# A transformer block and a two-layer mixer on one core: two-operand work moved from Pool to VectorE, and the feed-forward norm's root applied behind the up-products

## The chip, the core and the metric

One core of a Trainium2 chip runs the whole program. Its engines are TensorE (PE in the profile; its weight loads are PEld), VectorE (DVE), ScalarE (ACT), GpSimd (POOL, called Pool here) and SyncE (SP), which issues most DMAs. The metric is the device time of one execution in microseconds, as the median of several runs. Beside it there is one profiled execution, with every instruction's start and duration.

## What is computed

512 tokens of 1024 features go through a first block (mixer and feed-forward) and then through two layers of a second block. All is float32. Cut to what the change touches:

```python
def rms_norm(x, g):
    return x * lax.rsqrt(jnp.mean(x * x, axis=-1, keepdims=True) + 1e-6) * g

# first block
h = rms_norm(x, norm_mix_pre); proj = h @ w_in        # queries, keys, values, pool, memory queries, gates
mix = gate0 * y_attn + gate1 * y_pool + gate2 * y_mem
x = x + rms_norm(mix @ w_out, norm_mix_post)
h2 = rms_norm(x, norm_ffn_pre)
up = causal_depthwise_conv(h2 @ w_up, conv_w, conv_b)  # 3 taps along the tokens, 2 x 2816 features
g, v = split(up); ff = (gelu(g) * v) @ w_down
x = x + rms_norm(ff, norm_ffn_post)
# second block, layer 0: attention of 16 heads over the tokens and 256 context tokens, rotary positions, silu gates
# second block, layer 1: neighbourhood attention of 8 heads beside a depthwise convolution of 31 taps, a layer norm
#   and silu; then the last norm
```

The root of `h2`'s norm is one number for each token. A product over the features commutes with it: (x g r) @ W = r ((x g) @ W).

## The kernel before, in words

Features lie on the 128 partitions, tokens along the free dimension: x is 8 tiles of 128 x 512. Every weight product (`Product`, line 438) makes one 128 x 512 tile of results. It loads 128 x 1024 weights (`raw`), splits them into a high part on ACT (`whi`, line 458) and a low part, `raw - whi` (`wlo`, line 460), and makes 8 x 3 matmuls: high by high, high by low, low by high. Moving operands are split in the same way (`split`, line 488, `split_scaled`, line 492). Two buffers each hold the weights' parts, so the split of one product lies beside the matmuls of the product before it.

PE works in program order, and the program is written out by a planner in Python that counts microseconds of matmuls (`clock`). `advance`, `steps` and `run` issue matmuls of a batch; `defer(us, f)` calls f after so many microseconds of them; `background` holds work of other engines, given out at `rate` items per microsecond; `weave` puts products between the steps of attention; `drain` gives out the rest. The other engines take their instructions in their own order, DVE and Pool among them, and DMAs are issued by SP in order (a few by ACT).

Pool has these two-operand operations before the change: weights' low parts wherever `low_parts_on(G)` holds (lines 693 to 701 and 1541 to 1545: the start, and the latents' attention of layer 0); every third block's square sum with `SumSq(T, True)` (line 552); low parts of every third block in `norm_to` (line 582); the sums of the multiscale pool (line 717); the mix's additions (line 851); six of eight additions to x in `post_norm` (line 1418); two of four rotary products (lines 1068, 1070); gating and low parts in `lat_apply` (lines 1517, 1518); the last 13 of 31 taps of the depthwise convolution (`NTAP`, lines 1711 to 1717), each an ACT copy with a scale and a Pool addition to `ub`, which line 1723 merges; two sums of the layer norm (line 1731); every third product of the last norm (line 1787). Pool also has operations with one tensor operand, which stay: the scaling of scores by their sums (lines 775, 921, 1131) and of the bias (line 1648).

At the end of the first block's mixer the output products run (`outs`), then `post_norm` adds their normed result to x block by block, then the second root is made (`rms_now`, line 571: sums over the features on PE, nine small DVE steps in `rsqrt`, a spread by PE) and `norm_to` makes `h2` from x, gain and root. Meanwhile PE does the context's products (`filler`). Then x is stored to DRAM (`spill_x`), and the 44 up-products, 24 down-products and the context's attention follow, woven. An up-product's result is taken up by `conv3`: ACT scales it and adds the bias, and two DVE operations add the earlier tokens' taps, all three from PSUM:

```python
            S.activation(out=o, in_=ps, func=AF.Identity, scale=vc("conv_w", 88 + ct), bias=vc("conv_b", ct))
            V.scalar_tensor_tensor(out=o[:, 1:], in0=ps[:, :T - 1], scalar=vc("conv_w", 44 + ct), in1=o[:, 1:],
                                   op0=ALU.mult, op1=ALU.add)
```

Two PSUM banks take products' results at that time (`set_banks(2, 2)`).

Of the kernel before, what the change touches and what calls it, by code (L numbers as in the profile page):

```python
# [14 lines left out]
ALU = mybir.AluOpType  # L15
# [16 lines left out]
NTAP = 13   # convolution taps on the Pool engine  # L32
# [160 lines left out]
class Blocks:  # L193
    """[128, kt, n] as a tile for each of the kt blocks"""
# [8 lines left out]
def body(nc, tc, A, out, dbg=None):  # L203
# [75 lines left out]
    lo_engines = deque()  # L279

    def low_parts_on(*engines):
        lo_engines.clear()
        lo_engines.extend(engines)

    low_parts_on(V)
# [31 lines left out]
    # Products come in batches, which run in the order in which they were added. The weights of the next two are under way  # L317
    # while one runs.
# [69 lines left out]
    def lazy(weights, n, products):  # L388
        """the products of these weights, which products() gives when the first one starts"""
# [12 lines left out]
    def when(ready, products):  # L402
        """the products, not before ready()"""
# [21 lines left out]
    def need(ready):  # L425
        """more of the woven batch until ready()"""
# [4 lines left out]
    # ------------------------------------------------ products in three passes of float32r parts  # L431
# [6 lines left out]
    class Product:  # L438
        """one tile of a product, then evac(psum). cols: columns of the operand; keep: (pool, buffers) for the weights'
        parts; same: an earlier product with the same weights"""  # L440
# [11 lines left out]
        def parts(self):  # L452
            if self.same:
                self.hi, self.lo = self.same.hi, self.same.lo
            elif self.hi is None:
# [3 lines left out]
                lo_engines.rotate(-1)  # L459
                lo_engines[-1].tensor_tensor(out=self.lo[:, :n], in0=self.raw[:, :n], in1=f32(self.hi[:, :n]), op=ALU.subtract)  # L460
# [27 lines left out]
    def split(src, hi, lo, eng=None):  # L488
        S.copy(out=hi, in_=src)  # L489
        (eng or V).tensor_tensor(out=lo, in0=src, in1=f32(hi), op=ALU.subtract)  # L490
# [8 lines left out]
    def token_sums(accs, n, sel=None):  # L499
        """accs, each [128 features, n tokens] -> sums over the features (by the columns of sel), tokens on partitions"""  # L500
# [1314 lines left out]
```

## Time and profile before

| | us |
|---|---|
| three runs | 1807.56, 1810.9, 1818.63 |
| median | 1810.9 |
| profiled execution, first to last instruction | 1808.9 |
| PE busy / DVE busy / ACT busy / POOL busy in it | 1684.3 / 1278.4 / 902.7 / 390.0 |

Of the profiled execution's own time the profile gives the span alone. Busy time of an engine is the time in which at least one of its instructions ran; successive instructions of one engine overlap a little in the record, and matmuls are pipelined, so PE's busy time is not PE at its peak. PEclk is the share of the full TensorE clock that was granted.

### The profile page before, as it was taken

Reading aid. Unit: us, or ns where it says so; the run is one execution under the profiler, and the core shown is the slowest. Engines: PE = TensorE matmul, PEld = TensorE weight load, DVE = VectorE, ACT = ScalarE, POOL = GpSimd, SP = SyncE. Lnnn points to the kernel's source line nnn. Section 1 sums busy time; section 2 is a strip of 40 time slices with the busy share of each in tenths; the row PEclk is TensorE's granted clock in tenths of the full one; section 3 lists DMA queues with packets and bytes.
Section 4 is the critical chain, followed back from the end, with each engine's and each line's share of the span. In section 5 each row is a group of like instructions: output and inputs, shape, how many; then the busy total and the mean of one; then the engine's idle time right before and its main releaser. Section 6 shows DMA issues by size and latency. Waiting matters only on the chain. (4 is left out here: it accounts for less than half of the span.)

```text
span 1808.9 us, 25065 instructions
## 1 busy us (share of the span) xinstructions
PE 1684.3 (93%) x8756; PEld 1407.0 (78%) x8756; DVE 1278.4 (71%) x2474; ACT 902.7 (50%) x1700; POOL 390.0 (22%) x364
## 2 busy tenths in 40 slices
PE   7899999999998889999999998999988989888797
PEld 7788888888776768888778777778877787777677
DVE  6678766777597676644664767677778667888774
ACT  5443225555423456654763433366767445565452
POOL 3320111010021210000000002145544004656400
PEclk8999999999999999999999999999999999999898
DMA  5435555544364432333333556232321554243141
GB/s 197 136 121 176 162 164 151 135 122 117 126 202 161 148 103 94 123 118 105 111 100 110 193 163 211 84 103 70 78 64 47 186 172 137 82 120 97 35 140 59
DMA packets 84878, 227.10 MB, mean 126 GB/s; under 512 B 12048, under 2 KB 24720, under 8 KB 84752
## 3 DMA queue, kind: packets, MB, share of 16 engines
q1 hardware_dynamic: 82880, 220.51, 39.3%
q10 hardware_dynamic: 1872, 4.98, 0.9%
q8 instruction: 70, 1.15, 0.3%
q14 instruction: 56, 0.46, 0.1%
HBM read 181.93 MB, written 9.44 MB: 106 GB/s over the span
## 5 line engine op out<-in xcount | busy, mean ns | idle before, releaser
L294 PE MATMUL mm<-hh,whi 128*128 128x512 f32 (+1 forms) x1120 | 442.2, 395 | 16.6 <-DVE tg L593 4.6
L458 ACT CAST whi<-raw 128x1024 fp32r<-128x1024 f32 (+2 forms) x264 | 268.4, 1017 | 378.7 <-PE mm L294 326.8
L294 PE MATMUL mm<-hh,wlo 128*128 128x512 f32 (+1 forms) x1120 | 424.1, 379 | 6.4 <-DVE wlo L460 6.4
L294 PE MATMUL mm<-hl,whi 128*128 128x512 f32 (+1 forms) x1120 | 424.5, 379 | 3.4 <-DVE hl L490 1.7
L460 DVE TENSOR_TENSOR wlo<-raw,whi 128x1024 fp32r<-128x1024 f32 (+2 forms) x245 | 309.9, 1265 | 151.1 <-ACT whi L458 147.2
L294 PEld LDWEIGHTS mm<-hh,whi 128*128 128x128 f32 x1120 | 216.6, 193 | 51.4 <-DVE tg L593 6.1
L294 PEld LDWEIGHTS mm<-hh,wlo 128*128 128x128 f32 x1120 | 215.2, 192 | 48.8 <-DVE wlo L460 7.8
L294 PEld LDWEIGHTS mm<-hl,whi 128*128 128x128 f32 x1120 | 216.3, 193 | 34.2 <-DVE hl L997 2.7
L1131 POOL TENSOR_SCALAR sb<-sb,l 128x256 f32<-128x256 f32 (+3 forms) x128 | 106.3, 832 | 453.8 <-DVE l L1130 377.6
L294 PE MATMUL mm<-h2h,whi 128*128 128x512 f32 x352 | 141.8, 403 | 4.0 <-DVE cv L1342 3.0
L490 DVE TENSOR_TENSOR ptl<-tr,pth 128x512 fp32r<-128x512 f32 (+2 forms) x240 | 115.6, 497 | 41.8 <-ACT pth L489 40.0
L489 ACT CAST pth<-tr 128x512 fp32r<-128x512 f32 (+2 forms) x240 | 100.3, 436 | 89.8 <-PE tr L586 88.3
L294 PE MATMUL mm<-h2l,whi 128*128 128x512 f32 x352 | 140.1, 398 | 3.5 <-POOL h2l L490 2.1
L294 PE MATMUL mm<-h2h,wlo 128*128 128x512 f32 x352 | 139.7, 397 | 0.8 <-DVE wlo L460 0.8
L586 PE MATMUL tr<-c,sb 128*128 128x128 f32 x624 | 107.5, 282 | 25.1 <-DVE ptl L490 12.8
L586 PEld LDWEIGHTS tr<-c,sb 128*128 128x128 f32 x624 | 78.9, 145 | 52.0 <-issue 10.3
L810 DVE CUSTOM_DVE_ANT_0 mj<-mraw,cb 128x1024 f32<-128x1024 f32 x88 | 111.1, 1263 | 1.2 <-DMA mraw<-in_mod_w 0.5
L1126 ACT ACTIVATE sb<-sb,mn 128x512 f32<-128x512 f32 (+1 forms) x64 | 49.7, 776 | 70.7 <-DVE mn L1122 51.6
L1710 DVE SCALAR_TENSOR_TENSOR mixf<-up,vec,mixf 128x512 f32<-128x512 f32 x68 | 80.9, 1189 | 1.0 <-ACT mixf L1708 0.2
L294 PEld LDWEIGHTS mm<-h2l,whi 128*128 128x128 f32 x352 | 66.4, 189 | 19.2 <-POOL h2l L490 3.2
L294 PEld LDWEIGHTS mm<-h2h,whi 128*128 128x128 f32 x352 | 66.3, 188 | 19.2 <-issue 4.0
L1717 POOL TENSOR_TENSOR ub<-ub,ta 128x512 f32<-128x512 f32 x48 | 78.9, 1644 | 7.8 <-ACT ta L1716 5.1
(374 smaller groups left out, 3303.6 us busy)
## 6 DMA issues: line engine op xcount, KB each, us to landing
raw<-in_w_in SPq DMA_DIRECT2D x56, 512.0 KB, 3.4
mraw<-in_mod_w SPq DMA_DIRECT2D x48, 512.0 KB, 3.4
raw<-in_w_up SPq DMA_DIRECT2D x44, 512.0 KB, 3.4
raw<-in_ev_w SPq DMA_DIRECT2D x40, 512.0 KB, 3.4
raw<-in_od_w SPq DMA_DIRECT2D x36, 512.0 KB, 3.5
qd<-hl SPq DMA_DIRECT2D x48, 256.0 KB, 5.1
raw<-in_w_d SPq DMA_DIRECT2D x16, 512.0 KB, 3.3
raw<-in_ev_o SPq DMA_DIRECT2D x16, 512.0 KB, 3.4
```

The source lines that it names most:

```text
L294: on_pe(nc.tensor.matmul(ps, l, r, start=start, stop=stop), max(n * 0.00042, 0.107) * (2 if l.dtype == F32 else 1))
L458: S.copy(out=self.hi[:, :n], in_=self.raw[:, :n])
L460: lo_engines[-1].tensor_tensor(out=self.lo[:, :n], in0=self.raw[:, :n], in1=f32(self.hi[:, :n]), op=ALU.subtract)
L489: S.copy(out=hi, in_=src)
L490: (eng or V).tensor_tensor(out=lo, in0=src, in1=f32(hi), op=ALU.subtract)
L586: on_pe(nc.tensor.transpose(out=ps[:, k * P:(k + 1) * P], in_=src(b), identity=ident), 0.107)
L810: tc.keep_in_program_order(V.tensor_tensor_reduce(out=jk, in0=raw, in1=cb[:, n, :], scale=0.5, scalar=0.0, op0=ALU.mult, op1=ALU.add, accu ...
L1126: S.activation(out=sb, in_=src, func=AF.Exp, scale=-1.0, bias=mn, accum_out=l[:, 0:1])
L1131: G.tensor_scalar(out=sb, in0=sb, scalar1=l[:, 0:1], scalar2=0.0, op0=ALU.mult, op1=ALU.add)
L1710: V.scalar_tensor_tensor(out=u[m], in0=up[:, j:j + T], scalar=wc(j), in1=u[m], op0=ALU.mult, op1=ALU.add)
L1717: G.tensor_tensor(out=st["ub"], in0=st["ub"], in1=pj, op=ALU.add)
```

## The change

It does two things. First, all two-operand work of Pool named above is VectorE's; `low_parts_on`, `NTAP`, the second accumulator of `SumSq` and the `eng` argument of `split` are gone, and all 30 taps of the depthwise convolution after the first are one DVE chain. A very small copy in the multiscale pool goes the other way, from VectorE to Pool. Second, `post_norm` makes `h2`'s parts from x and the gain alone, in the same loop, and the root multiplies each up-product's result in `conv3`; results that come before the root wait in `unrooted`. With it, the filler runs to its end before x is stored, `h2` and the feed-forward's accumulator take the first block's buffers (`hp`), and the table `base` is loaded before the differential attention rather than at the start. (Comments are gone too.)

```diff
 Product.parts
-                lo_engines.rotate(-1)
-                lo_engines[-1].tensor_tensor(out=self.lo[:, :n], in0=self.raw[:, :n], in1=f32(self.hi[:, :n]), op=ALU.subtract)
+                V.tensor_tensor(out=self.lo[:, :n], in0=self.raw[:, :n], in1=f32(self.hi[:, :n]), op=ALU.subtract)
 norm_to
-            split(t, dst.h[:, k, :], dst.l[:, k, :], G if k % 3 == 1 else V)
+            split(t, dst.h[:, k, :], dst.l[:, k, :])
 pool_sums
-                G.tensor_tensor(out=nx[:, sh:], in0=cur[:, sh:], in1=cur[:, :T - sh], op=ALU.add)
-                V.tensor_copy(out=nx[:, :sh], in_=cur[:, :sh])
+                V.tensor_tensor(out=nx[:, sh:], in0=cur[:, sh:], in1=cur[:, :T - sh], op=ALU.add)
+                G.tensor_copy(out=nx[:, :sh], in_=cur[:, :sh])
 next_branch
-        G.tensor_tensor(out=mixacc[:, m, :], in0=mixacc[:, m, :], in1=t, op=ALU.add)
+        V.tensor_tensor(out=mixacc[:, m, :], in0=mixacc[:, m, :], in1=t, op=ALU.add)
 feed-forward
+    root, unrooted = [], []
+
+    def rooted_up(r):
+        root.append(tl(fp, [P, T], "root", 1))
+        S.copy(out=root[0], in_=r)
+        for f in unrooted:
+            f()
+
     def conv3(ct, then):
-        def evac(ps):
-            o = tl(fp, [P, T], "cv", 3)
-            S.activation(out=o, in_=ps, func=AF.Identity, scale=vc("conv_w", 88 + ct), bias=vc("conv_b", ct))
-            V.scalar_tensor_tensor(out=o[:, 1:], in0=ps[:, :T - 1], scalar=vc("conv_w", 44 + ct), in1=o[:, 1:],
+        def scaled(ps):
+            t, o = tl(fp, [P, T], "cu", 1), tl(fp, [P, T], "cv", 3)
+            V.tensor_tensor(out=t, in0=ps, in1=root[0], op=ALU.mult)
+            S.activation(out=o, in_=t, func=AF.Identity, scale=vc("conv_w", 88 + ct), bias=vc("conv_b", ct))
+            V.scalar_tensor_tensor(out=o[:, 1:], in0=t[:, :T - 1], scalar=vc("conv_w", 44 + ct), in1=o[:, 1:],
                                    op0=ALU.mult, op1=ALU.add)
...
+        def evac(ps):
+            if root:
+                scaled(ps)
+            else:
+                unrooted.append(lambda: scaled(ps))
...
-    def post_norm(y, r, gname, filler, us=0.8):
-        ss = SumSq(T, True)
+    def post_norm(y, r, gname, filler, us=0.8, after=lambda k: None):
+        ss = SumSq(T)
         for k in range(KD):
             V.scalar_tensor_tensor(out=y[:, k, :], in0=y[:, k, :], scalar=vc(gname, k), in1=r, op0=ALU.mult, op1=ALU.mult)
-            (V if k % 4 == 3 else G).tensor_tensor(out=xs[k], in0=xs[k], in1=y[:, k, :], op=ALU.add)
+            V.tensor_tensor(out=xs[k], in0=xs[k], in1=y[:, k, :], op=ALU.add)
+            after(k)
             advance(filler, us)
...
+    h = pair(hp, "h")
+
+    def gained(k):
+        split_scaled(xs[k], vc("norm_ffn_pre", k), h.h[:, k, :], h.l[:, k, :])
+
-    ss = post_norm(y, ss.rms_now(filler, e=4 * EPS), "norm_mix_post", filler)
-    b1.close()
-    fst = ExitStack()
-    fp = pool(fst, "fp")
-    h = pair(fp, "h2")
-    advance(filler, B1A)
-    norm_to(xs, "norm_ffn_pre", ss.rms_now(filler), h, T, filler)
+    ss = post_norm(y, ss.rms_now(filler, e=4 * EPS), "norm_mix_post", filler, after=gained)
+    run(filler)
     xd = spill_x("xd0")
     xst.close()
+    fst = ExitStack()
     fp = pool(fst, "ff")
-    y = tl(fp, [P, KD, T], "y", 1)
-    run(filler)
+    y = tl(hp, [P, KD, T], "acc", 1)
+    defer(1.5, lambda: ss.rms(rooted_up))
     steps(second, 24)
 lat_apply
-        G.tensor_tensor(out=mixf[:, m, :], in0=mixf[:, m, :], in1=sg, op=ALU.mult)
-        defer(2.5, lambda: split(mixf[:, m, :], mix.h[:, m, :], low(m), V if m == 7 else G))
+        V.tensor_tensor(out=mixf[:, m, :], in0=mixf[:, m, :], in1=sg, op=ALU.mult)
+        defer(2.5, lambda: split(mixf[:, m, :], mix.h[:, m, :], low(m)))
 convolution: tap
-                elif j < 31 - NTAP:
+                else:
                     V.scalar_tensor_tensor(out=u[m], in0=up[:, j:j + T], scalar=wc(j), in1=u[m], op0=ALU.mult, op1=ALU.add)
-                elif j == 31 - NTAP:
-                    st["ub"] = tl(ep, [P, T], "ub", 1)
-                    S.activation(out=st["ub"], in_=up[:, j:j + T], func=AF.Copy, scale=wc(j))
-                else:
-                    pj = tt()
-                    S.activation(out=pj, in_=up[:, j:j + T], func=AF.Copy, scale=wc(j))
-                    G.tensor_tensor(out=st["ub"], in0=st["ub"], in1=pj, op=ALU.add)
...
-            background.append(lambda: V.tensor_tensor(out=u[m], in0=u[m], in1=st["ub"], op=ALU.add))
```

Left out are the rotary products, the layer norm's sums, the square sums and the last norm's products, where `G.` becomes `V.` in the same way; the last norm reads the root from PSUM for all eight products, and ACT's copy of it (line 1783) goes.

## Rows read from the trace of the kernel before

**Rows 1.** the page, part 1: busy us (share of the span) x instructions of each engine
```profile
PE 1684.3 (93%) x8756; PEld 1407.0 (78%) x8756; DVE 1278.4 (71%) x2474; ACT 902.7 (50%) x1700; POOL 390.0 (22%) x364
```

**Rows 2.** busy us by stretch: length, PE, PEld, DVE, ACT, POOL, PE clock, DMA, GB/s
```profile
0.00:60.00 60.00, 44.23 (x277) 41.26 (x278) 41.32 (x75) 30.75 (x57) 23.70 (x16) 0.89 0.57 189
470.00:560.00 90.00, 85.37 (x361) 67.34 (x361) 77.48 (x119) 26.96 (x41) 15.76 (x8) 0.97 0.58 187
603.00:660.00 57.00, 44.79 (x291) 39.94 (x290) 45.84 (x97) 27.58 (x49) 15.15 (x10) 0.91 0.43 139
660.00:1098.00 438.00, 430.01 (x2089) 353.32 (x2088) 266.16 (x449) 233.96 (x372) 16.04 (x32) 1.00 0.38 123
1098.00:1150.00 52.00, 41.95 (x251) 36.40 (x250) 39.92 (x61) 21.16 (x29) 9.81 (x7) 0.93 0.51 177
1187.00:1410.00 223.00, 200.45 (x1257) 173.66 (x1256) 172.84 (x417) 151.93 (x356) 112.82 (x97) 0.98 0.29 77
1494.00:1712.00 218.00, 189.18 (x967) 154.26 (x966) 184.96 (x286) 125.78 (x242) 124.71 (x104) 0.95 0.35 98
```

**Rows 3.** costliest groups by shape, 1661 to 1678 us, DVE and POOL (busy, mean ns | idle)
```profile
L1710 DVE SCALAR_TENSOR_TENSOR mixf<-up,vec,mixf 128x512 f32<-128x512 f32 x7 | 10.3, 1471 | 0.1
L1717 POOL TENSOR_TENSOR ub<-ub,ta 128x512 f32<-128x512 f32 x10 | 16.1, 1609 | 3.1 <-ACT ta L1716 2.5
```

**Rows 4.** the same view, 1684 to 1704 us
```profile
L1710 DVE SCALAR_TENSOR_TENSOR mixf<-up,vec,mixf 128x512 f32<-128x512 f32 x8 | 6.1, 759 | 0.0
L1131 POOL TENSOR_SCALAR sb<-sb,l 128x640 f32<-128x640 f32 x3 | 5.1, 1716 | 4.9 <-DVE l L1130 4.9
```

**Rows 5.** the same view, 470 to 560 us
```profile
L460 DVE TENSOR_TENSOR wlo<-raw,whi 128x1024 fp32r<-128x1024 f32 x13 | 24.6, 1893 | 0.5 <-ACT whi L458 0.5
L851 POOL TENSOR_TENSOR acc<-acc,tg 128x512 f32<-128x512 f32 x8 | 15.8, 1970 | 76.0 <-DVE tg L850 76.0
```

**Rows 6.** the same view, 100 to 190 us, DVE
```profile
L460 DVE TENSOR_TENSOR wlo<-raw,whi 128x1024 fp32r<-128x1024 f32 x9 | 11.1, 1236 | 10.1 <-ACT whi L458 10.1
```

**Rows 7.** the same view, whole span, DVE
```profile
L1340 DVE SCALAR_TENSOR_TENSOR cv<-mm,vec,cv 128x511 f32<-128x511 f32 x44 | 32.9, 747 | 13.6 <-ACT cv L1339 13.6
L1352 DVE TENSOR_TENSOR cv<-cv 128x512 f32<-128x512 f32 x22 | 15.1, 686 | 0.2
```

**Rows 8.** the same view, 603 to 660 us, DVE
```profile
L552 DVE TENSOR_TENSOR sqa<-sqa,ta 128x512 f32<-128x512 f32 x6 | 5.8, 970 | 0.0
L581 DVE SCALAR_TENSOR_TENSOR ta<-x,vec,tr 128x512 f32<-128x512 f32 x8 | 5.8, 739 | 0.0
```

**Rows 9.** order of time, ACT and SP, 604 to 668 us (start, us, what)
```profile
659.21 0.77 ACT L1339 ACTIVATE cv<-mm,vec 128x512 f32<-128x512 f32 x1
614.96 2.84 SPq L1308 DMA_DIRECT2D xd<-x  x3
```

**Rows 10.** costliest groups by shape, 1494 to 1712 us, DVE
```profile
L1710 DVE SCALAR_TENSOR_TENSOR mixf<-up,vec,mixf 128x512 f32<-128x512 f32 x68 | 80.9, 1189 | 1.0 <-ACT mixf L1708 0.2
L460 DVE TENSOR_TENSOR wlo<-raw,whi 128x1024 fp32r<-128x1024 f32 x22 | 29.8, 1354 | 9.7 <-ACT whi L458 9.6
L1723 DVE TENSOR_TENSOR mixf<-mixf,ub 128x512 f32<-128x512 f32 x4 | 3.4, 841 | 0.0
```

**Rows 11.** whom PE waited for, 1494 to 1712 us (total us, times, longest us)
```profile
PE tr L294 <- DVE ptl L490: 11.1, 8, 2.4
PE tr L586 <- DVE ptl L490: 7.7, 8, 2.3
PE tr L586 <- DVE mixf L1163: 6.7, 4, 2.1
```

**Rows 12.** costliest groups by shape, 1187 to 1410 us, POOL
```profile
L460 POOL TENSOR_TENSOR wlo<-raw,whi 128x1024 fp32r<-128x1024 f32 x12 | 29.1, 2424 | 10.9 <-ACT whi L458 10.8
L1517 POOL TENSOR_TENSOR mixf<-mixf,tg 128x512 f32<-128x512 f32 x8 | 10.4, 1296 | 6.4 <-DVE mixf L1163 5.9 <-DVE tg L593 0.5
```

**Rows 13.** whom PE waited for, 1187 to 1410 us
```profile
PE tr L586 <- POOL sb L1131: 4.2, 3, 1.6
```

More of the change, by code (lines that the diff above doesn't have):

```diff
@@ L31 @@
 NOT = 1
-NTAP = 13
 TH = 3
@@ L486, in by_halves, with split @@
         return ps + a + b
-    def split(src, hi, lo, eng=None):
+    def split(src, hi, lo):
         S.copy(out=hi, in_=src)
-        (eng or V).tensor_tensor(out=lo, in0=src, in1=f32(hi), op=ALU.subtract)
+        V.tensor_tensor(out=lo, in0=src, in1=f32(hi), op=ALU.subtract)
     def split_scaled(src, scale, hi, lo):
@@ L536, in body, with __init__ @@
     class SumSq:
-        def __init__(self, n, two=False, p=None):
-            self.n, self.two, self.p, self.accs, self.k = n, two, p, [], 0
+        def __init__(self, n, p=None):
+            self.n, self.p, self.accs = n, p, []
         def add(self, ap, cols=slice(None)):
-            i = 1 if self.two and self.k % 3 == 2 else 0
-            self.k += 1
-            if i == len(self.accs):
+            if not self.accs:
                 self.accs.append(tl(self.p, [P, self.n], "sqb", 1) if self.p else tl(tmp, [P, T], "sqa", 2)[:, :self.n])
-                S.activation(out=self.accs[i], in_=ap, func=AF.Square)
+                S.activation(out=self.accs[0], in_=ap, func=AF.Square)
             else:
-                sq, acc = tt(ap.shape[-1]), self.accs[i][:, cols]
+                sq, acc = tt(ap.shape[-1]), self.accs[0][:, cols]
                 S.activation(out=sq, in_=ap, func=AF.Square)
-                (G if i else V).tensor_tensor(out=acc, in0=acc, in1=sq, op=ALU.add)
+                V.tensor_tensor(out=acc, in0=acc, in1=sq, op=ALU.add)
             return self
@@ L683, in body @@
     load_fm(xin, A["x"])
-    base = tl(hp, [P, T], "base", 1)
-    nc.scalar.dma_start(out=base, in_=A["c1"][:, 197:709])
     for k, ap in enumerate(ks(memx)):
@@ L692, in body @@
     defer(SM, lambda: mss.rms(roots))
-    low_parts_on(G)
     advance(filler, SX)
-    ss = SumSq(T, True).add_all(ks(xin))
+    ss = SumSq(T).add_all(ks(xin))
     advance(filler, SA)
@@ L975, in body @@
     aos = ExitStack()
-    ao = pair(pool(aos, "ao"), "ao")
+    aop = pool(aos, "ao")
+    ao = pair(aop, "ao")
+    base = tl(aop, [P, T], "base", 1)
+    nc.scalar.dma_start(out=base, in_=A["c1"][:, 197:709])
     dst = ExitStack()
@@ L1067, in finish @@
                 V.tensor_tensor(out=a[0], in0=xf[0], in1=cos, op=ALU.mult)
-                G.tensor_tensor(out=a[1], in0=xf[1], in1=sin, op=ALU.mult)
+                V.tensor_tensor(out=a[1], in0=xf[1], in1=sin, op=ALU.mult)
                 V.tensor_tensor(out=a[2], in0=xf[0], in1=sin, op=ALU.mult)
-                G.tensor_tensor(out=a[3], in0=xf[1], in1=cos, op=ALU.mult)
+                V.tensor_tensor(out=a[3], in0=xf[1], in1=cos, op=ALU.mult)
                 defer(RG, lambda: turned(a))
@@ L1334, in body @@
     ff = {}
-    def conv3(ct, then):
-        def evac(ps):
-            o = tl(fp, [P, T], "cv", 3)
-            S.activation(out=o, in_=ps, func=AF.Identity, scale=vc("conv_w", 88 + ct), bias=vc("conv_b", ct))
-            V.scalar_tensor_tensor(out=o[:, 1:], in0=ps[:, :T - 1], scalar=vc("conv_w", 44 + ct), in1=o[:, 1:],
+    root, unrooted = [], []
[4 more added lines that the diff above has]
+            f()
+    def conv3(ct, then):
+        def scaled(ps):
[3 more added lines that the diff above has]
+            V.scalar_tensor_tensor(out=o[:, 1:], in0=t[:, :T - 1], scalar=vc("conv_w", 44 + ct), in1=o[:, 1:],
                                    op0=ALU.mult, op1=ALU.add)
-            V.scalar_tensor_tensor(out=o[:, 2:], in0=ps[:, :T - 2], scalar=vc("conv_w", ct), in1=o[:, 2:],
+            V.scalar_tensor_tensor(out=o[:, 2:], in0=t[:, :T - 2], scalar=vc("conv_w", ct), in1=o[:, 2:],
                                    op0=ALU.mult, op1=ALU.add)
             then(o)
+        def evac(ps):
[3 more added lines that the diff above has]
+                unrooted.append(lambda: scaled(ps))
         return product(A["w_up"][ct], lambda: h, evac)
@@ L1475, in body @@
     fst.close()
+    b1.close()
     evp = pool(evs, "evp")
@@ L1708, in tap @@
                     S.activation(out=u[m], in_=up[:, 0:T], func=AF.Identity, scale=wc(0), bias=vc("dw_b", m))
-                elif j < 31 - NTAP:
+                else:
                     V.scalar_tensor_tensor(out=u[m], in0=up[:, j:j + T], scalar=wc(j), in1=u[m], op0=ALU.mult, op1=ALU.add)
-                elif j == 31 - NTAP:
-                    st["ub"] = tl(ep, [P, T], "ub", 1)
-                    S.activation(out=st["ub"], in_=up[:, j:j + T], func=AF.Copy, scale=wc(j))
-                else:
-                    pj = tt()
-                    S.activation(out=pj, in_=up[:, j:j + T], func=AF.Copy, scale=wc(j))
-                    G.tensor_tensor(out=st["ub"], in0=st["ub"], in1=pj, op=ALU.add)
-            nv = 31 - NTAP
-            order = [j for a, b in zip(range(nv), chain(range(nv, 31), [None] * 31)) for j in (a, b) if j is not None]
-            order += [j for j in range(31) if j not in order]
-            background.extend([lambda j=j: tap(j) for j in order])
-            background.append(lambda: V.tensor_tensor(out=u[m], in0=u[m], in1=st["ub"], op=ALU.add))
+            background.extend([lambda j=j: tap(j) for j in range(31)])
             if m == 3:
@@ L1730, in layer_norm @@
         s1, s2 = tl(tmp, [P, T], "sqa", 2), tl(tmp, [P, T], "sqa", 2)
-        G.tensor_tensor(out=s1, in0=u[0], in1=u[1], op=ALU.add)
-        G.tensor_tensor(out=s2, in0=u[2], in1=u[3], op=ALU.add)
+        V.tensor_tensor(out=s1, in0=u[0], in1=u[1], op=ALU.add)
+        V.tensor_tensor(out=s2, in0=u[2], in1=u[3], op=ALU.add)
         def mean():
@@ L1781, in scaled @@
     def scaled(r, cs):
-        rs = tl(tmp, [P, T], "sqa", 2)[:, :C]
-        S.copy(out=rs, in_=r)
         for k in range(KD):
             t = tt(C) if k % 2 else tg(C)
-            if k % 3 == 2:
-                G.tensor_tensor(out=t, in0=xs[k][:, cs], in1=rs, op=ALU.mult)
-            else:
-                V.tensor_tensor(out=t, in0=xs[k][:, cs], in1=r, op=ALU.mult)
+            V.tensor_tensor(out=t, in0=xs[k][:, cs], in1=r, op=ALU.mult)
             nc.sync.dma_start(out=out[k][:, cs], in_=t)
```

8 lines of the change are left out of this document (removed).

## The prediction, made before the changed kernel ran

> **What bounds the kernel now.** I read the page's first part, then busy time by stretch, then the groups by shape in stretches with and without work on Pool, then whom PE waited for. PE is busy 93% of the span, DVE 71%, Pool 22% [rows 1]: at most some 125 us can be won, and only where PE stands still. By stretch [rows 2] PE's idle time (length less busy) is 15.8 us at the start (the wait for the first data among it), 4.6 in 470 to 560, 12.2 in 603 to 660 (between mixer and feed-forward), 8.0 in the feed-forward, 10.1 in 1098 to 1150, 22.6 in the latents' attention of layer 0 and 28.8 in layer 1's. The clock row adds to that: 0.91 over 603 to 660 means 0.09 of 57 us, 5.1 us of full-speed work, lost at the lower of the two levels.
>
> The reader should then set DVE's instructions against Pool's. A tap takes 1471 ns while Pool adds taps of its own [rows 3] and 759 ns twenty microseconds later, when Pool only scales scores [rows 4]. The low part of a weight takes 1893 ns where Pool adds to the mix [rows 5] and 1236 where it doesn't [rows 6]. So a two-operand operation on Pool stretches DVE's two-operand operations beside it. Per us of it: 7 x 0.712 = 5.0 us in 16.1 us of Pool [rows 3], 0.31; and 13 x 0.657 = 8.5 us in 15.8 [rows 5], 0.54. One Pool addition of 1.3 to 2.0 us thus costs DVE 0.4 to 1.1 us, as much as doing the addition itself: 0.686 us [rows 7]. The Trainium skill (SBUF — State Buffer, Who interferes with whom) says that an instruction of VectorE with two SBUF inputs and one of GpSimd that reads SBUF share a read interface, and that the second fully blocks until the first ends. By that each collision costs the whole of the other; the rows give 0.31 to 0.54 of it, since not every DVE operation beside it has two SBUF inputs.
>
> **The change part by part.** DVE's price of a moved operation is 0.686 us for 512 columns [rows 7], 1.236 for a weight [rows 6].
>
> Start, 0 to 60: 7 weights' low parts, 3 low parts of the norm and a sum of squares come to DVE, 7 x 1.236 + 4 x 0.686 = 11.4 us; the 23.7 us of Pool [rows 2] that go give back 0.31 to 0.54 of that, 7.3 to 12.8. DVE ends between 1.4 less and 4.1 more. But a weight is split in 1.24 us rather than in about 2.4 (the same operation of Pool, [rows 12]), and PE waits on these. Taken: -2 us, from -5 to +2. The table for the causal bias (256 KB) is loaded later, behind the memory stage: nothing, its first use is some 20 us further on.
>
> 470 to 560: 8 additions, 8 x 0.686 = 5.5 us, against 8.5 us of stretching that goes [rows 5]. DVE, with 77.5 of 90 us [rows 2], has 3.0 us less to do. PE's 4.6 idle us here lie beside a DVE that is 86% busy, so I take DVE's gain: -3, from -6 to 0. The other eight mix additions (about 190 to 260) and the sums of the multiscale pool lie where PE is never idle: nothing.
>
> 603 to 660, the norm: six additions to x and one of squares come to DVE, 7 x 0.686 = 4.8 us. Of the norm, 8 products with gain and root (0.739 each, [rows 8]) and 8 subtractions (0.686; 5 of them on DVE) become 8 operations of 0.747 [rows 7]: DVE has 5.9 + 3.4 - 6.0 = 3.3 us less. Relief: 15.15 us of Pool x 0.31 to 0.54 = 4.7 to 8.2. So DVE goes from 45.8 to between 39 and 43 us. More weighs that the root leaves the way: now sum, nine small steps, spread and eight operations on DVE stand between x and the first up-product, whose result is taken up at 659.2 us [rows 9]; then only the eight gained parts do, and the root has a whole product (24 matmuls) of time. Late next is DVE itself, still busy for some 40 of the 57 us; so of PE's 12.2 idle and 5.1 clocked-away us I take a third: -6, from -12 to 0. The eight stores of x (about 0.35 us of issue each on SP: three in 2.84 with gaps, [rows 9]) move behind the context's products, among loads of weights: nothing, at worst +3.
>
> Feed-forward: each of 44 results is multiplied by the root first: 44 x 0.686 = 30.2 us on DVE, from 266 to 296 of 438 us [rows 2], 68%. PE covers it: a pair of products gives DVE far less than it takes PE, and the bank is free after 0.69 us instead of one ACT and two DVE operations (2 x 0.747, [rows 7], plus 0.77, [rows 9]). The single scratch tile makes the next result wait for the two taps before it: 0.69 + 0.77 + 1.5 = 3.0 us in a chain, under the 5 to 6 us of a product (438 us over 44 up-products and 24 down-products, attention among them: 6.4 on average). Taken: 0, from -4 to +8; without the cover up to 30.
>
> 1098 to 1150: seven operations, 4.8 us, against 9.81 x 0.31 to 0.54 = 3.0 to 5.3: -0.5, from -3 to +3.
>
> Latents, 1187 to 1410: 12 weights [rows 12], 8 gatings [rows 12], 7 low parts and 6 rotations: 12 x 1.236 + 21 x 0.686 = 29.2 us to DVE; Pool loses about 29.1 + 21 x 1.296 = 56.3 us, relief 17.5 at the lower ratio. DVE goes from 172.8 to 184.5 of 223 us, 78 to 83%. Against that PE's waits on Pool, 4.2 us [rows 13], should go: scaling no longer stands in Pool's queue behind a weight of 2.4 us. Behind DVE's longer queue stand the low parts of probabilities and the gates, for which PE waits too; no operation there is stretched any more. I take -4, from -10 to +10.
>
> Layer 1, 1494 to 1712: DVE takes 52 more taps. 52 x 0.759 = 39.5, less 68 x (1.189 - 0.759) = 29.2 for those that it has, less 3.4 for the four merges, less 22 x (1.354 - 1.236) = 2.6 for weights [rows 4, 6, 10]: +4.3, from 185.0 to 189.3 of 218 us. That is no gain on DVE. But ACT loses 52 copies and Pool some 80 us, and PE's waits, 25.5 us in 20 [rows 11], each end behind an operation of DVE in order; if a stretched tap before each is shorter by half of 0.43 us, that is 20 x 0.2 = 4. Taken: -4, from -12 to +10.
>
> The tail's four multiplications: 0, within 1.
>
> Sum: -2 - 3 - 6 + 0 - 0.5 - 4 - 4 + 0 = -19.5 on the profiled span of 1808.9: 1789.4. That span is the only time the profile gives; the runs' median, 1810.9, is 2.0 above it. So 1791.4, say 1791.
>
> **Rivals.** *DVE's longer queue eats the attention gains.* DVE is at 83% and 87% in the two attentions by my own sums, and every low part waits in its order. Then -4 and -4 become +1 each: 1801. For it: DVE's work doesn't fall there; against: its longest operations do.
>
> *The root's wait only moves.* The sum over features is put into the first up-product, after 1.5 us of it, and PE does it in order: if the last squares are late, PE stands there, with x's additions now all on DVE. The -6 goes: 1797.
>
> *More comes loose.* Without Pool's two-operand work the attentions lose half of their 51.4 idle us instead of 8: 1791 - 17 = 1774. For it: Pool is busy for 113 and 125 us there [rows 2], in front of the scaling; against: 20 of layer 1's waits are on DVE [rows 11].
>
> *The lock stays (slower).* Pool still scales all scores from SBUF in layer 1. If that stretches a tap as Pool's additions did, to 1.471 us [rows 3], the 120 taps cost 120 x 0.712 = 85 us more; DVE's 189 become 274, 56 over the stretch's 218: 1791 + 56 = 1847. It decides from a tap of about 1.0 us on, where DVE fills the stretch (29 us over 120 taps). Against it, taps took 759 ns beside such scaling while the scaling itself took 1716 ns [rows 4]: Pool waits there, not DVE. For it speaks the rule of the Trainium skill named above (SBUF — State Buffer, Who interferes with whom), which asks of GpSimd's instruction only that it reads SBUF.
>
> **How the numbers follow.** A change under 1% can hardly be told from none; 1% of 1810.9 is 18.1, so the bounds are 1792.8 and 1829. The sum as forecast 0.45, of which 0.29 lie below 1792.8; the queue 0.20, all within 1%; the root's wait 0.15, 0.03 of it below; more loose 0.12, faster; the lock 0.08, slower. Faster 0.44, same 0.48, slower 0.08. Two bounds of single terms at once (-6 and -8 in the attentions, or +14 in one with a lost boundary) give 1775 to 1812; with the case of 1774 the range is 1771 to 1814, and it leaves out the lock and little else.
>
> **What would show it.** Right: no two-operand operation on Pool; weights' low parts at about 1.24 us everywhere; taps near 0.76 and 120 of them, DVE's busy time in layer 1 about as before; the first up-result taken up some 6 us sooner against the start of the outputs' norm, with a higher clock there; the feed-forward as long as before with 30 us more on DVE; no PE wait on Pool in the latents. Wrong: taps over 1 us; PE waiting on the squares in the first up-product; new waits of PE on DVE's root products or on low parts in the attentions; scaling on Pool that takes twice as long and ends PE's waits.

## The result and the profile after

The changed kernel takes 1778.76 us (median of 4 runs, 1776.85 to 1781.23) against 1809.23 for the kernel before (4 runs): a ratio of 0.9829, 95% interval 0.9806 to 0.9852, so 30 us or 1.7% faster. The forecast was 1791, the range 1771 to 1814.

First the page of the changed kernel: busy time by engine, then DVE's, POOL's and the clock's rows over 40 slices of the span.

```profile
span 1775.1 us, 24940 instructions
...
PE 1667.1 (94%) x8732; PEld 1400.2 (79%) x8732; DVE 1307.0 (74%) x2648; ACT 873.3 (49%) x1647; POOL 172.9 (10%) x229
...
DVE  6778666777588587655785777678888765999975
...
POOL 0120000000000000000000000013222101233200
PEclk9999999999999989999999999999999999999899
```

Against [rows 1] Pool has lost 217 us of work and DVE has gained only 29, though it does 174 more instructions. Near the end DVE shows 9 in four slices running: layer 1.

To see where the 33.8 us of span went I cut both traces at the same pieces of work. Each product's matmul by a weight's low part occurs 2072 times in both kernels in the same order; a stage runs from the start of one of them to that of another. The first two columns are the stage's ends in the trace before (us), the third the change in its length, the fourth the forecast's term for it.

```
from     to       after - before   forecast   stage
0        485.9    +0.2             -2         start, and up to the differential attention
485.9    598.3    -3.7             -3         branches and mix (470 to 560, and what follows)
598.3    689.1    -3.4             -6         norm between mixer and feed-forward
689.1    1075.3   -3.0              0         feed-forward
1075.3   1159.0   +1.3             -0.5       norm behind it
1159.0   1419.2    0.0             -4         latents' attention
1419.2   1510.2   +0.3              0
1510.2   1726.4  -24.2             -4         layer 1
1726.4   1808.9   -1.4              0         tail
```

Stages that two kernels have in common, instruction for instruction, differ by up to 4 us among the traces of this study (the first stage by 6, the stage 1075.3 to 1159.0 by 7), so a single 1 or 2 in this table means nothing, and a 3 only with a row behind it or the same change in several traces. Layer 1 is 24 of the 34.

Next, layer 1 of either kernel cut into six equal parts (start:end and length, then busy us of PE, PEld, DVE, ACT, POOL; PE clock; DMA; GB/s). Before:

```profile
1510.20:1546.20 36.00, 31.75 (x162) 25.98 (x161) 32.84 (x44) 22.67 (x42) 27.92 (x22) 0.95 0.33 94
1546.20:1582.30 36.10, 31.53 (x171) 25.98 (x170) 31.00 (x46) 22.59 (x43) 20.77 (x20) 1.00 0.29 88
1582.30:1618.30 36.00, 32.66 (x172) 26.76 (x171) 31.24 (x52) 21.62 (x43) 19.02 (x20) 1.00 0.49 134
1618.30:1654.40 36.10, 30.89 (x158) 24.71 (x157) 33.20 (x50) 19.56 (x38) 24.40 (x20) 0.95 0.44 115
1654.40:1690.40 36.00, 31.29 (x152) 25.23 (x150) 33.68 (x49) 23.06 (x43) 25.00 (x18) 0.91 0.16 54
1690.40:1726.40 36.00, 29.28 (x153) 24.30 (x154) 23.03 (x49) 14.94 (x34) 6.15 (x6) 0.86 0.09 30
sum 216.20, PE 187.38 PEld 152.96 DVE 184.99 ACT 124.45 POOL 123.25; mean PE 31.23 PEld 25.49 DVE 30.83 ACT 20.74 POOL 20.54
```

After:

```profile
1501.90:1534.00 32.10, 32.10 (x173) 26.92 (x172) 28.94 (x53) 18.02 (x35) 8.12 (x11) 1.00 0.50 139
1534.00:1566.00 32.00, 31.90 (x177) 26.92 (x176) 31.66 (x57) 16.17 (x32) 9.66 (x12) 1.00 0.37 110
1566.00:1598.00 32.00, 32.00 (x176) 26.94 (x175) 31.83 (x59) 15.65 (x31) 10.21 (x11) 1.00 0.35 105
1598.00:1630.00 32.00, 30.17 (x165) 25.06 (x164) 31.46 (x60) 16.13 (x33) 11.62 (x11) 1.00 0.50 140
1630.00:1662.00 32.00, 25.38 (x140) 20.60 (x138) 31.86 (x61) 15.76 (x31) 4.05 (x6) 0.96 0.10 34
1662.00:1694.00 32.00, 26.55 (x139) 22.83 (x140) 26.61 (x52) 12.17 (x26) 6.45 (x4) 0.88 0.15 50
sum 192.10, PE 178.09 PEld 149.26 DVE 182.36 ACT 93.89 POOL 50.11; mean PE 29.68 PEld 24.88 DVE 30.39 ACT 15.65 POOL 8.35
```

Before, PE stood idle some 3 to 7 us in every sixth, 28.8 in all (216.2 less 187.4). After, it is full in the first half, and 14.0 us of idle time are left, 12.1 of them in the last third. The other 9.3 us of the 24.1 are PE's busy time itself, for the same products and attention. A part of it goes with the clock: each busy time multiplied by the clock of its row, the six add up to 177.4 us before and 173.9 after. So some 6 of the 9.3 us are the clock, which stood at 0.95, 0.95 and 0.91 in the first, fourth and fifth part before and stands at 1.00, 1.00 and 0.96 now. What the other 3 to 4 are was not found. DVE has as much to do as before, in 24 us less: it is now busy for 182 of 192 us.

The costliest groups of DVE in that stretch after the change (busy us, mean ns | idle before):

```profile
L1714 DVE SCALAR_TENSOR_TENSOR mixf<-up,vec,mixf 128x512 f32<-128x512 f32 x120 | 93.9, 782 | 0.9
L451 DVE TENSOR_TENSOR wlo<-raw,whi 128x1024 fp32r<-128x1024 f32 x21 | 25.7, 1224 | 0.7 <-ACT whi L450 0.7
```

And whom PE waited for in it (us in total, times, longest):

```profile
PE tr L574 <- DVE ptl L481: 9.6, 7, 4.4
PE tr L286 <- DVE ptl L481: 3.4, 4, 1.5
PE tr L574 <- DVE mixf L1150: 0.8, 1, 0.8
```

A tap takes 782 ns against 1189, so the 120 taps (93.9 us) take only 13 us more than the 68 before the change (80.9, [rows 10]). The three waits of [rows 11], 25.5 us in 20, are the same kinds still: 13.8 in 12.

### The profile page after: what moved, and what is told of

Its sections match the earlier page's. It is cut to its first block, busy times and chain, and to the rows that moved or that the text cites. A ratio compares the mean times of both kernels' runs of the same rounds, so it can differ in the third digit from the quotient of the medians.

```text
span 1775.1 us, 24940 instructions
## 1 busy us (share of the span) xinstructions
PE 1667.1 (94%) x8732; PEld 1400.2 (79%) x8732; DVE 1307.0 (74%) x2648; ACT 873.3 (49%) x1647; POOL 172.9 (10%) x229
## 5 line engine op out<-in xcount | busy, mean ns | idle before, releaser
L286 PE MATMUL mm<-hh,whi 128*128 128x512 f32 (+1 forms) x1472 | 581.7, 395 | 18.6 <-DVE tg L581 4.7
L286 PE MATMUL mm<-hh,wlo 128*128 128x512 f32 (+1 forms) x1472 | 561.9, 382 | 9.6 <-DVE wlo L451 9.6
L286 PE MATMUL mm<-hl,whi 128*128 128x512 f32 (+1 forms) x1472 | 561.9, 382 | 1.6 <-DVE hl L984 1.6
L286 PEld LDWEIGHTS mm<-hh,wlo 128*128 128x128 f32 x1472 | 280.4, 191 | 68.4 <-DVE wlo L451 11.9
L286 PEld LDWEIGHTS mm<-hh,whi 128*128 128x128 f32 x1472 | 281.6, 191 | 65.9 <-DVE tg L581 5.9
L286 PEld LDWEIGHTS mm<-hl,whi 128*128 128x128 f32 x1472 | 282.0, 192 | 45.7 <-DVE hl L984 2.9
L574 PEld LDWEIGHTS tr<-c,sb 128*128 128x128 f32 x624 | 78.2, 144 | 45.1 <-POOL sb L1118 10.1
L1714 DVE SCALAR_TENSOR_TENSOR mixf<-up,vec,mixf 128x512 f32<-128x512 f32 x120 | 93.9, 782 | 0.9
L286 PE MATMUL s<-kp,qd 128*128 128x256 f32 (+3 forms) x320 | 77.0, 339 | 0.7 <-ACT sb L1113 0.7
L286 PE MATMUL mm<-ffh,whi 128*128 128x512 f32 x176 | 70.3, 400 | 1.1 <-ACT ffh L480 1.1
L286 PE MATMUL mm<-ffl,whi 128*128 128x512 f32 x176 | 69.8, 397 | 0.2 <-DVE ffl L481 0.2
L286 PE MATMUL mm<-ffh,wlo 128*128 128x512 f32 x176 | 69.7, 396 | 0.0
```

Of the source, the lines that this page charges most:

```text
L286: on_pe(nc.tensor.matmul(ps, l, r, start=start, stop=stop), max(n * 0.00042, 0.107) * (2 if l.dtype == F32 else 1))
L574: on_pe(nc.tensor.transpose(out=ps[:, k * P:(k + 1) * P], in_=src(b), identity=ident), 0.107)
L1714: V.scalar_tensor_tensor(out=u[m], in0=up[:, j:j + T], scalar=wc(j), in1=u[m], op0=ALU.mult, op1=ALU.add)
```

## The experiments

Ratios are to the kernel before, in runs on the same chip. The changes of a stage are those of the table's cuts, each trace against that of the kernel before.

**Part A alone.** The kernel before with all two-operand work of Pool on VectorE.

```
-    low_parts_on(G)
+    low_parts_on(V)
-                (G if i else V).tensor_tensor(out=acc, in0=acc, in1=sq, op=ALU.add)
+                V.tensor_tensor(out=acc, in0=acc, in1=sq, op=ALU.add)
...
```

> Part A alone: all two-operand work of Pool on VectorE, the feed-forward's root as before. The changed kernel gained 24 us in layer 1, 3.6 in 470 to 560, 3.3 at the norm between mixer and feed-forward and 3.0 in the feed-forward. Theory: layer 1 and 470 to 560 belong to this part, the other two to the root, so about 28 us faster than before (1781), the norm stage as long as before, the feed-forward too. Rival: the norm stage too gains by Pool's leaving (15 us of Pool work lie there), so 31 us faster (1778). A second rival: the parts lean on each other, and this one alone gives under 20 us.

Measured: 1785.97, ratio 0.9861 (0.9843 to 0.9879), 25 us faster. Layer 1 is 23.1 us shorter, the branches (485.9 to 598.3) 3.8. The norm stage is 3.4 us *longer*, the feed-forward within 1 of before. So the first theory holds for three stages, and the rival (the norm gains by Pool's leaving) is turned round.

**Part B alone.** Only the root and its norm, Pool's work as before.

```
-            S.activation(out=o, in_=ps, func=AF.Identity, scale=vc("conv_w", 88 + ct), bias=vc("conv_b", ct))
+            V.tensor_tensor(out=t, in0=ps, in1=root[0], op=ALU.mult)
+            S.activation(out=o, in_=t, func=AF.Identity, scale=vc("conv_w", 88 + ct), bias=vc("conv_b", ct))
...
```

> Part B alone: the root multiplied onto the up-products' results, Pool's work as before. Theory: 3 us in the feed-forward (banks are free after one operation instead of three) and 3 to 7 at the norm, so 1803 to 1805, same within 1%. Rival: the root has nothing to do with the norm stage's gain, which then comes from Pool: 1807 and the stage as long as before. Slower than before if the 44 more operations on DVE are stretched by Pool's in this stretch; Pool does little there, so not expected.

Measured: 1807.28, ratio 0.9981 (0.9963 to 0.9999), 3 us faster. The feed-forward is 4.8 us shorter, the norm stage by 0.4 only. So the theory holds for the feed-forward and not for the norm.

Whom PE waited for in the feed-forward, kernel before (689.1 to 1075.3 us), its first row:

```profile
PE mm L294 <- DVE cv L1342: 3.7, 5, 1.2
```

The same stage with the root alone has no such wait:

```profile
PE mm L294 <- DVE wlo L460: 2.2, 2, 1.2
PE mm L294 <- ACT ffh L489: 1.1, 1, 1.1
PE mm L294 <- ACT whi L458: 1.0, 1, 1.0
PE mm L294 <- DVE ffl L490: 0.2, 1, 0.2
```

In the kernel before a product's bank was held until the second convolution step on DVE had read it; now until one multiplication has. With part A alone the same row of 3.7 us in 5 waits is still there; in the changed kernel it is gone. PE's idle time in the stage falls with it, from 7.5 to 4.8 us in the changed kernel, and DVE is busy for 24.3 us more (257.3 against 232.9). All eight traces with the root behind the products agree: the stage is 2.7 to 4.8 us shorter than before in them, and between 0.5 longer and 2.2 shorter in those without.

The norm stage gains only with both parts, and the waits do not say why. Whom PE waited for in it, first rows, part A alone (596.7 to 690.9 us):

```profile
PE tr L294 <- DVE ta L513: 6.9, 1, 6.9
PE mm L294 <- DVE wlo L460: 3.6, 2, 3.2
```

The changed kernel (594.8 to 682.2 us), all rows:

```profile
PE mm L286 <- DVE wlo L451: 5.2, 2, 4.1
PE tr L286 <- DVE ta L504: 4.3, 1, 4.3
PE mm L286 <- ACT ta L539: 3.0, 1, 3.0
PE tr L286 <- DVE rs_y L516: 0.5, 1, 0.5
```

The row with ta is a spread of roots by head, of the context's queries, for which PE waits while DVE does the norm's work; it was 1.9 us before, in 2, and is 4.5 with part B alone. With Pool's additions on DVE and the norm's sixteen operations still ahead of the first up-product (part A alone) it grows to 6.9. With the root off the way the waits on the parts of the norm, which were 2.1 and 1.4 us before, are gone, but waits of the same size came earlier in the stage: PE's idle time in it is 12.6 us before, 15.7 with part A, 11.1 with part B and 13.0 with both. Part A alone loses 3.4 us, part B alone gains 0.4, both together gain 3.4. So the changed kernel's 3.4 are not idle time won. They lie in PE's busy time, 74.4 us against 78.2 (78.6 and 79.3 with one part), at the same clock of 0.94 (0.89 and 0.91 with one part). About 1 us of that is one accumulator of squares less, 16 small matmuls for its sums instead of 24; the rest is open. These are single traces; the stage's length in the six later variants of the changed kernel, which leave it as it is, is 0.6 to 3.5 shorter than before, so the order of the three stands and the size of the gain is rough.

**Only the convolution's taps on VectorE.** The kernel before with that one edit.

```
-                elif j < 31 - NTAP:
+                else:
                     V.scalar_tensor_tensor(out=u[m], in0=up[:, j:j + T], scalar=wc(j), in1=u[m], op0=ALU.mult, op1=ALU.add)
-                elif j == 31 - NTAP:
...
-                    G.tensor_tensor(out=st["ub"], in0=st["ub"], in1=pj, op=ALU.add)
```

> Only the convolution's taps moved from Pool to VectorE (52 taps more on DVE, 52 copies less on ACT, 48 additions and 4 merges gone). Theory: the whole gain of layer 1 hangs on this, 22 to 24 us, so about 1786, and the other stages stand as before. Rival: the gain is spread over the kernel's phase in layer 1 (layer norm's sums, weights that come differently out of the latents), and the taps alone give half of it, about 1797.

Measured: 1786.03, ratio 0.9855 (0.9833 to 0.9876); layer 1 is 24.2 us shorter, exactly as with everything changed, and no other stage is shorter by more than 3.0. The theory holds: of part A's dozen places this one gives as much as all of them together (0.9861), as far as the times can tell. 0.9855 times 0.9981 is 0.9836, within the interval of the whole change.

**Which of Pool's effects was it?** Three kernels from the one before take parts of the taps' path away. In the first, Pool's additions go and the copies on ACT stay:

```
                     S.activation(out=pj, in_=up[:, j:j + T], func=AF.Copy, scale=wc(j))
-                    G.tensor_tensor(out=st["ub"], in0=st["ub"], in1=pj, op=ALU.add)
```

> The kernel before with Pool's 48 additions of taps left out (the last 12 taps of each convolution are then missing from the result); the 52 copies on ACT and the 68 taps and 4 merges on DVE stay. Takes away both the stretching of DVE and the occupation of Pool's queue, and leaves ACT as it was. If stretching or Pool's queue holds layer 1 up: at least 24 us faster than before, 1785 or less (DVE has 36 us less to do than in the changed kernel). If ACT's copies in front of exponentials and probabilities hold it up: under 12 us faster, about 1798.

Measured: 1776.58, ratio 0.9813 (0.9775 to 0.9850). Layer 1 is 33.4 us shorter, with ACT as busy as before (123.9 against 124.5 us). The stretch in one row:

```profile
1508.80:1691.60 182.80, 174.93 (x961) 147.85 (x960) 151.37 (x285) 123.88 (x240) 43.65 (x55) 0.99 0.34 101
```

The additions of the kernel before (1491.3 to 1726.4 us), and the taps without them:

```profile
L1717 POOL TENSOR_TENSOR ub<-ub,ta 128x512 f32<-128x512 f32 x48 | 78.9, 1644 | 7.8 <-ACT ta L1716 5.1
```

```profile
L1710 DVE SCALAR_TENSOR_TENSOR mixf<-up,vec,mixf 128x512 f32<-128x512 f32 x68 | 54.8, 806 | 1.0 <-ACT mixf L1708 0.2
```

Taking Pool's 48 additions away and nothing else takes 33.6 us off DVE's busy time (185.0 to 151.4), 26.1 of them off the 68 taps (80.9 to 54.8). The changed kernel, with the 52 taps, has 31.0 us more on DVE than this one (182.4) and is 9.3 us slower in layer 1. So the change is worth -33.4 by what Pool no longer does and +9.3 by what DVE does instead.

How this reaches PE can be counted in the traces. Most of PE's waits in layer 1 are on `ptl`, the low parts of the probabilities. One can be made as soon as ACT has made the high part; from that moment to their start on DVE the 56 of this stage stand 74.4 us in all in the kernel before, 48 of them behind taps. In the changed kernel it is 51.9 us, 29 of them behind taps, and without the additions 23.2 and 12. DVE is busy with other work for all but 1 us of each sum.

In the second, Pool's queue stays full, but with operations of one operand:

```
-                    G.tensor_tensor(out=st["ub"], in0=st["ub"], in1=pj, op=ALU.add)
+                    G.tensor_scalar(out=pj, in0=pj, scalar1=1.0, scalar2=0.0, op0=ALU.mult, op1=ALU.add)
```

> As the kernel before, but each of the 48 additions on Pool is a multiplication by a constant of the same 128x512 tile (one operand; the last 12 taps are missing from the result). Pool's queue stays occupied, and no two-operand operation of Pool lies beside DVE's. Theory (stretching): taps at about 0.76 us and most of the 24 us gained. Rival (Pool's queue in front of the scaling of scores): the wait from the reciprocal to the scaling stays at about 0.54 us on average, and the gain is under 10 us.

Measured: 1780.31, ratio 0.9842 (0.9798 to 0.9886). Layer 1 is 29.1 us shorter although Pool is busy there for 85.6 us against 43.7 without those operations:

```profile
L1710 DVE SCALAR_TENSOR_TENSOR mixf<-up,vec,mixf 128x512 f32<-128x512 f32 x68 | 61.0, 897 | 1.0 <-ACT mixf L1708 0.2
...
L1717 POOL TENSOR_SCALAR ta<-ta 128x512 f32<-128x512 f32 x48 | 42.9, 911 | 11.1 <-ACT ta L1716 11.0
```

So 29 of 33 us go with the kind of the operation alone. But these take 0.91 us each instead of 1.64, and so Pool's queue is shorter as well: a scaling starts 0.21 us after the reciprocal that it needs from DVE on average, against 0.54 in the kernel before and 0.19 without the additions. This run does not tell the two-operand kind from a full queue. The waits speak against the queue: of PE's 28.8 idle us in layer 1 before, 25.5 end behind DVE [rows 11] and 3.0 behind ACT, none behind Pool's scaling. The rows behind those of [rows 11]:

```profile
PE tr L294 <- ACT sb L1126: 2.0, 1, 2.0
PE mm L586 <- ACT tg L1027: 1.0, 1, 1.0
```

The taps are at 897 ns, against 806 without these operations: one-operand work stretches them too, a little.

In the third the copies on ACT and the four merges go as well:

```
-            background.extend([lambda j=j: tap(j) for j in order])
+            background.extend([lambda j=j: tap(j) for j in range(18)])
...
```

> As the one before, and the 52 copies on ACT left out too (18 of 31 taps are done). Against it the price of the copies alone is seen: 0 to 3 us by the theory that DVE's stretched taps cost the time, 10 or more if ACT's queue does. And against the changed kernel the price of 52 more taps on DVE: if DVE's length bounds layer 1, this one is some 15 us faster than the changed kernel's layer 1; if not, under 5.

Measured: 1786.98, ratio 0.9877 (0.9838 to 0.9916), *slower* than with the copies, which neither theory expected. Its last sixth of layer 1, and that of the kernel with the copies:

```profile
1670.70:1702.80 32.10, 27.03 (x125) 22.90 (x126) 16.72 (x38) 10.76 (x22) 0.96 (x2) 0.73 0.24 81
```

```profile
1661.20:1691.60 30.40, 25.24 (x139) 21.06 (x140) 19.27 (x41) 12.17 (x27) 5.88 (x5) 0.94 0.10 36
```

The granted clock is 0.73 there against 0.94: 27 us of busy PE do less work than 25. Leaving the copies out also puts the remaining taps one behind the other in the list that is spread over the products, so they come sooner and end sooner. Why this leads to a lower clock at the end was not settled; the run can't serve to price the copies. The next one does.

**ACT's relief.** The changed kernel with 52 copies put back beside the taps.

```
                     V.scalar_tensor_tensor(out=u[m], in0=up[:, j:j + T], scalar=wc(j), in1=u[m], op0=ALU.mult, op1=ALU.add)
+                    if j % 2 == 0 and j < 28:
+                        S.activation(out=tt(), in_=up[:, j:j + T], func=AF.Copy, scale=wc(j))
```

> The changed kernel with 52 copies on ACT put back beside the taps (their results are used by nothing). ACT's queue as before, Pool's and DVE's as in the changed kernel. If ACT's relief is a part of layer 1's gain, 5 us or more slower than the changed kernel (1784 or more); if only stretching counts, under 2 us (1779 to 1781).

Measured: 1780.21, ratio 0.9845 (0.9801 to 0.9888); layer 1 is 1.7 us longer than in the changed kernel. ACT's relief is worth about 2 us at most.

**The latents.** The changed kernel with 12 weights' low parts on Pool again.

```
     set_banks(1, 3)
+    lo_eng[0] = G
     weave(attention([it for n in range(16) for it in lat_items(n)], LL, True), filler, LR, LZ, 4)
     run(filler)
+    lo_eng[0] = V
```

> The changed kernel with the weights' low parts on Pool again during the latents' attention (12 weights; gatings, low parts of the mix and rotations stay on DVE). The latents' stage lasted as long after the change as before, where I had counted 4 us of gain. If two opposite terms cancel there (relief of Pool's queue against DVE's longer one), going back halfway shows one of them: 2 us or more either way in that stage. If neither is on the path: within 1.5 us, 1777 to 1781.

Measured: 1784.46, ratio 0.9858 (0.9821 to 0.9896), an interval that overlaps that of the changed kernel; the latents' stage is 2.4 us longer than there. That is over the 2 us named above, and longer than in all seven other traces with the changed code of this stage (1.6 shorter to 0.7 longer than before, this one 2.5 longer); PE's idle time is 26.0 us against 23.3. But kernels that share that stage's code differ by up to 3.8 in it, so a single trace is a hint and no more: the low parts on Pool may cost 2 to 3 us there, which something else of the change then takes back.

**What bounds layer 1 now?** In its last third PE idles for 12 us and no independent product is left. Four attempts to use that, all on the changed kernel. The first convolution ahead of the attention's first products:

```
-    firsts = Batch(lazy([A["od_w"][ct] for ct in (12, 16, 20)], T, lambda: na_products(0)))
+    firsts = Batch(lazy([A["od_w"][ct] for ct in (4, 0, 12, 16, 20)], T, lambda: chain(convolution(0), na_products(0))))
```

> The changed kernel, but the first convolution's two products run ahead of the attention's first three, so that taps start about 19 us of products earlier, where DVE is busy for 5.7 to 10.4 of 15 us. In the changed kernel DVE is busy for 182 of layer 1's 192 us (from the fourth product on), while PE is full in its first two thirds and idle for 12 in its last third. Theory (DVE's work now sets layer 1's length): 4 to 10 us faster than the changed kernel, 1769 to 1775. Rival (the independent products are spent too early, DVE is only late where PE has nothing else): with two products fewer to stand in, no gain or some us slower, 1779 or more.

Fewer steps of products for each step of attention:

```
-NR = 1.85
+NR = 1.6
```

> The changed kernel with 1.6 instead of 1.85 steps of independent products for each step of layer 1's attention, so that they last longer. Theory (DVE's work sets the length): nothing won, within 3 us of the changed kernel, or a few lost since the last convolution starts later: 1777 to 1785. Rival (products spent too early): most of the 12 us of idle time in the last third goes, 1768 to 1773.

Both:

> Both: the first convolution ahead, and 1.6 steps. Theory (DVE's work): as with the convolution ahead alone or up to 3 us better, 1768 to 1775. Rival (products spent too early): better than either alone, under 1768.

Two gates' products moved from behind the attention into it:

```
-                   na_gate(0), na_gate(1), na_gate(2)))
+                   na_gate(0), na_gate(1), na_gate(2), conv_gate(0), conv_gate(1)))
```

> The changed kernel with the products of the convolution's first two gates moved from behind layer 1's attention to the end of the products that stand in during it. In the changed kernel PE is idle for 12 us in the last 64 us of that stage, where no independent product is left, with the clock at 0.96 and 0.88. Theory (in the last third PE waits for DVE only because it has nothing else to do): two products (about 19 us of PE) fill most of that, 5 to 10 us faster than the changed kernel, 1769 to 1774. Rival (DVE, busy for 182 of 192 us there, sets the length): the stage gets no shorter, since what moves ahead leaves its gap behind: 1776 to 1781.

Measured, in this order: 1780.13 (0.9842, interval 0.9796 to 0.9888), 1783.39 (0.9846, 0.9806 to 0.9885), 1777.98 (0.9822, 0.9781 to 0.9862), 1780.82 (0.9846, 0.9817 to 0.9876). None can be told from the changed kernel's 0.9829. Layer 1's stage is 2.9, 2.8 and 1.3 us longer in the first three; in the fourth it is 3.1 shorter and the next stage, where the gates are missed, 7.1 longer. Two of the fourth's rows at the same times (its stage starts and ends some 5 to 8 us sooner, at 1496.6 and 1685.6):

```profile
1630.00:1662.00 32.00, 28.54 (x143) 23.16 (x142) 30.44 (x58) 15.90 (x32) 5.42 (x5) 0.95 0.20 67
1662.00:1694.00 32.00, 25.19 (x127) 20.81 (x126) 20.72 (x43) 10.04 (x22) 5.69 (x4) 0.79 0.11 33
```

PE's gap is smaller in the one (3.5 us against 6.6) and wider in the other (6.8 against 5.5), with the clock at 0.79 there. So "the products are spent too early" falls, and so does the simple form of the other theory, that starting the taps earlier shortens the stage. What stands is the measured exchange above: DVE's amount of work in this stage counts, 9.3 us of time for 31.0 of DVE. Nothing found here beats the changed kernel.

## Why the prediction was right, and where it was not

The sign, the range and the mechanism in layer 1 (Pool's two-operand work slows DVE down) were right; the sizes of the terms were not. Layer 1's -24.2 lies outside its own bounds, -12 to +10, and all other terms, -15.5 in the forecast, gave -9.6. That 1778.8 lies so near to 1791 is in part luck: the two misses went opposite ways. Step by step:

- *A two-operand operation on Pool costs DVE beside it about as much as doing it.* Right. Here 48 additions (78.9 us) cost DVE 33.6, or 0.43 per us, between the 0.31 and 0.54 of the forecast. The low parts are at 1.22 to 1.23 us, and the lock (taps at 1.471 us beside scaling) is out: 782 ns, with Pool scaling as before. By the rule of the Trainium skill behind that rival (SBUF — State Buffer, Who interferes with whom) an instruction of VectorE with two SBUF inputs and one of GpSimd that reads SBUF contend for a lock, and the rule does not part GpSimd's instructions by the number of their operands. In these runs the number counts: one-operand operations cost DVE 0.18 us per us of Pool, two-operand ones 0.43 (worked out in the last section). What Pool lost on its own side was not measured, so the rule is not put to the test as a whole. The reason that the forecast gave for a price under the whole, that not every DVE operation has two SBUF inputs, no run shows.
- *Layer 1: DVE +4.3, time -4.* DVE's busy time came out 2.6 lower, the time at -24.2. The step that failed is "if a stretched tap before each is shorter by half of 0.43 us, that is 20 x 0.2 = 4". It took the relief of one tap ahead of each wait, where often several stand ahead (48 us of taps ahead of the 56 low parts), and it took the number of waits as given, where eight of 20 vanished (PE's idle time fell by 14.8 us). It also had no term for the clock, although [rows 2] showed 0.95 in this stretch; PE's busy time fell by 9.3, some 6 of them with the clock. "No gain on DVE" had been read as "no gain": DVE's total stayed, but what PE waits for stands 22.5 us less behind DVE's other work (51.9 against 74.4).
- *More comes loose* (1774) named this, for both attentions, at 0.12. It came true for one, and the time, 1778.8, lies between this case and the forecast. Its ground against it, that 20 waits were on DVE, was the reason for it: they were waits on a stretched DVE.
- *Latents -4.* Wrong, nothing came. "Scaling no longer stands in Pool's queue" did happen (it starts at most 0.2 us after its reciprocal, where it had been up to 3.0), but PE's waits on Pool did not go:

```profile
PE tr L574 <- POOL sb L1118: 4.8, 5, 1.8
PE mm L286 <- DVE tg L581: 4.7, 5, 1.4
```

  These are the first rows of 1180.0 to 1402.2 us in the changed kernel, against 4.2 us in 3 [rows 13]. A scaling of about 0.9 us is itself the last link before the transposes.
- *Norm stage -6.* -3.4, inside its bounds, but not by its reason. The step that failed is "of PE's 12.2 idle and 5.1 clocked-away us I take a third": in the table's stage the idle time went from 12.6 to 13.0 us, and the clock stayed at 0.94. The forecast also summed the root's gain and the moved additions, and they don't add: the root alone gives 0.4, the additions alone cost 3.4. The rival that the root's wait only moves is half seen. PE does not stand in the first up-product: between 639 and 652.3 us, with the root's sums and its spread in that time and the first up-product's result taken up at its end, it stands still for 0.55 us in all, where the kernel before stood 5.4 us from 645 us on. But 12.4 idle us now lie in the stage ahead of 639 us, against 7.1 before.
- *Feed-forward 0.* -3.0. The forecast had the fact ("the bank is free after 0.69 us instead of one ACT and two DVE operations") and gave it no price, though PE's 8.0 idle us there held 3.7 of waits on it.
- *470 to 560: -3.* -3.7, and -2.8 to -4.1 in all eight traces with these additions on VectorE, against 0 to -2.6 in the six without. *Start: -2.* +0.2: the low parts are at 1.22 us there, and PE did not gain by it.

## What to carry to other kernels

Read a wait on an engine together with what stretches that engine: a group whose mean differs between stretches (1471 and 759 ns) says that the waits on it can go without any of its work going. Moving work onto the busier engine won here because the work had slowed that engine down from where it was; a kernel that leaves the work out prices both halves (-33.4 and +9.3). And of a change in many places, ask which one carries it: one of part A's dozen gave all of layer 1's gain and as much as the dozen together (0.9855 and 0.9861).

## What was not expected of the hardware

Pool's one-operand operations stretch DVE's taps as well, less: with 42.9 us more of them the 68 taps went from 806 to 897 ns, 6.2 us in all or 0.14 us per us of Pool, against 0.33 for two-operand ones (1189 ns, 26.1 us for 78.9). Over all of DVE's work in layer 1 it is 7.6 us (159.0 against 151.4) or 0.18, against 0.43. In layer 1 DVE can be busy for 31.8 of 32 us, beside a PE that is busy for 32.0: there a full engine was no bound for the other by itself.
